# One layer of sparse attention and a state-space branch: Pool's front work on VectorE, and index scores in pieces of two PSUM banks and 2048 columns

## The chip, the cores and the metric

The kernel runs on one core of a Trainium2 chip, in one launch. The metric is the time of that launch on the device in microseconds. A core has five engines, each with its own queue of instructions worked off in order: TensorE (PE in the profile; PEld is its loading of weights), VectorE (DVE), ScalarE (ACT), Pool (POOL) and SyncE (SP), which only issues DMAs. They wait for one another by semaphores.

## What is computed

The layer takes x of 4096 positions by 1024 channels. Cut to what matters here, one projection gives the inputs of both branches, the attention branch selects 256 keys for each query, and both branches go through one output projection and a layer norm:

```python
proj = einsum('bsd,de->bse', x, w_in)
q, c_kv, q_idx, k_idx, w_idx, gate_a, u, gate_s = split(proj)
# index: 8 heads of 32 channels
idx_logits = einsum('bthd,bsd->bths', q_idx, k_idx)
index_score = einsum('bths,bth->bts', relu(idx_logits), w_idx)   # 4096 x 4096, causal
_, sel = top_k(index_score, 256)
# attention over the selected latents, 8 heads, keys and values absorbed
s = einsum('bthc,btkc->bthk', q_lat, c[sel]);  o_lat = softmax(s) @ c[sel]
# state-space branch: diagonal complex recurrence over positions, GELU, GLU
mixed = concat([att * silu(gate_a), ssm * silu(gate_s)])
out = layer_norm(2**0.25 * x + mixed @ w_out)
```

The kernel keeps float32 accuracy on TensorE by splitting an operand into a rounded high part and a remainder (hi and lo) and adding three products.

## The kernel before

The code is written as one stream, and a scheduler of the recording layer lays it out over the engines: for each engine it fixes an order in which instructions of later code stand between those of earlier code wherever it expects them to be ready. On the chip each queue then runs in that order.

**The first stage** holds two streams of work. The projections: `sweep(c, cols, following)` takes a chunk c of 512 positions through the 21 column blocks of COLS. Per block, 24 matmuls of 512 columns (`mm3`, L98 to L100) go to a PSUM tile ps_x (four of them), are evacuated through a staging tile `st` (four buffers) and stored to DRAM by SP. The first three blocks (index keys, index queries) run for all chunks at the start; the other 18 run later, chunk 7 first, which also rounds the weights into hi and lo (L498, L499) and stores them to w_d for the other chunks. Block ckv makes the normalised latent: it needs the squares (tile `sq`) and a diagonal matrix (L572, also `sq`). Block kv makes keys and values: 4 key pieces and 8 value pieces a chunk, each split into hi and lo by `split_pool`: ScalarE copies the PSUM tile twice, once rounded (L93) and once plain (L94), and Pool subtracts (L95). `prepare` transposes x for the next chunk and splits it with `split` (ScalarE rounds, L85, and VectorE subtracts straight out of PSUM, L87).

The selection: `select(group)` treats two to five tiles of 128 queries at once; tile i sees W = 128(i+1) keys. Tiles 0 and 1 need no selection. `score` (L233 to L258) computes the index scores: for each stretch of 1024 keys and each of 8 heads, two matmuls of 512 columns into PSUM tiles ps_i (four buffers of one bank), two relus on ScalarE (L248) into one tile `relu` of 1024 columns (four buffers), and one accumulation on VectorE (L257). Then eight rounds (L312 to L359) search each query's threshold: a count per tile, on VectorE (L321) or ScalarE (L317), and a dozen operations on a few columns. At the end of a group (L375 to L399), for each tile: ScalarE flips signs (L378), VectorE makes a mask of the entries above the threshold (L382), Pool adds it to the scores (L383), VectorE finds the eight largest of the rest and strikes them out (L385, L393), ScalarE turns the result into the mask (L397), and SP stores it. Score tiles of two groups fit, so a group's scoring lies beside the search of the one before it.

**The tail**: when the last group is selected, a check whether any row failed decides a branch; only then does the second stage begin.

**The second stage** is attention with the state-space branch between its instructions, then the output. Its code is not touched.

Pool's queue in the first stage also issues the loads of weights (L503) and of index queries (L238).

## Time and profile before

| | us |
|---|---|
| median of three runs | 4163.76 (4161.73 to 4170.51) |
| the profiled execution, whole | 4164.02 |
| its span, first to last instruction | 4162.0 |
| busy in the span: TensorE | 3715.5 |
| VectorE | 3445.4 |
| ScalarE | 2806.0 |
| Pool | 1907.0 |

Times in rows are counted from the start of the span. A row of lines names the source line, the engine, the operation, what it writes and reads, and the shape; then the count, the busy time in us and the mean of one instruction in ns; then the idle time of the engine just before these instructions, and what ended it. A line can be that of a helper: L87 is every subtraction of `split`. An instruction counts as busy from its start to its end, also while it stands still inside.

### The profile page before, as it was taken

The page shows a single profiled execution, that of the slowest core. Times are in us where ns is not written, and L with a number is a line of the kernel's source. Part 1 is how long each engine was busy: PE and PEld are TensorE (multiplying, and loading weights), DVE is VectorE, ACT ScalarE, POOL GpSimd, SP SyncE. Part 2 cuts the span into 40 slices and gives each one's busy share as a digit, 9 for nine tenths or more (in the row PEclk, how much of TensorE's full clock was granted, in tenths as well). Part 3 has the DMA queues.
Part 4 walks back from the last instruction along what each step waited for, and adds up shares of the span by engine and source line. Part 5 has one row for each costly group of instructions (what it writes and reads, how often), then busy time and mean ns, then how long its engine had stood idle before and what let it go on. Part 6 is the DMA issues. An engine that isn't in the chain of part 4 may idle for free.

```text
span 4162.0 us, 65556 instructions
## 1 busy us (share of the span) xinstructions
PE 3715.5 (89%) x20925; PEld 3123.2 (75%) x20925; DVE 3445.4 (83%) x7049; ACT 2806.0 (67%) x5100; POOL 1907.0 (46%) x3561
## 2 busy tenths in 40 slices
PE   6888988989889889319999999999999999899998
PEld 5666766766667667308988888889898989788887
DVE  4989999999998999859888888888888889665554
ACT  4677787766776767537777777777777778534342
POOL 1213443333332333336665757565657552344543
PEclk9898989989889999759999999999999999999999
DMA  8675867667676766434444544544545444544441
GB/s 230 156 203 165 269 187 222 188 190 210 169 213 180 210 198 188 123 100 125 130 134 130 147 134 140 134 132 127 138 119 153 114 137 134 164 141 139 136 128 71
DMA packets 521907, 656.26 MB, mean 158 GB/s; under 512 B 126800, under 2 KB 367952, under 8 KB 521552
## 3 DMA queue, kind: packets, MB, share of 16 engines
q1 hardware_dynamic: 438800, 448.54, 37.6%
q0 software_dynamic: 82752, 203.45, 18.2%
q8 instruction: 167, 2.74, 0.3%
q14 instruction: 188, 1.54, 0.1%
HBM read 480.61 MB, written 169.13 MB: 156 GB/s over the span
## 4 chain that ended last, share of the span: by engine, by line
PE 46%; ACT 3%; DMA 2%; DVE 1%; issue 1%; POOL 1%; SPq 0%; ACTq 0%; POOLq 0%; DVEq 0%
PE ps_t L1141 10%; PE ps_o L1153 6%; PE ps_o L1154 5%; PE ps_s L1108 5%; PE ps_s L1109 5%; PE ps_y L99 3%; PE ps_y L98 3%; PE ps_y L100 3%; ACT sc L1124 2%; PE ps L951 2%; PE ps_g L99 1%; PE ps_g L100 1%; PE ps_g L98 1%; DMA mb<-mask_d 1%; ACT ph L85 1%
## 5 line engine op out<-in xcount | busy, mean ns | idle before, releaser
L87 DVE TENSOR_TENSOR pl<-ps_t,ph 128x512 fp32r<-128x512 f32 x1088 | 748.2, 688 | 192.2 <-ACT ph L85 178.9
L85 ACT ACTIVATE ph<-ps_t 128x512 fp32r<-128x512 f32 x1088 | 643.6, 596 | 371.1 <-PE ps_t L1141 353.1
L1111 DVE CUSTOM_DVE_ANT_0 sc<-ps_s,mb 128x512 f32<-128x512 f32 (+3 forms) x1152 | 725.7, 638 | 38.4 <-PE ps_s L1109 19.4
L248 ACT ACTIVATE relu<-ps_i 128x512 f32<-128x512 f32 (+2 forms) x1136 | 586.2, 603 | 217.6 <-PE ps_i L247 146.8
L257 DVE SCALAR_TENSOR_TENSOR acc<-relu,wi,acc 128x1024 f32<-128x1024 f32 (+7 forms) x546 | 664.3, 1217 | 65.2 <-ACT relu L248 55.7
L1153 PE MATMUL ps_o<-ph,V 128*128 128x256 f32 x2176 | 658.7, 325 | 29.8 <-ACT ot L1157 26.8
L1141 PE MATMUL ps_t<-ident,sc 128*128 128x128 f32 x4352 | 654.5, 273 | 11.1 <-DVE pl L87 6.5
L1124 ACT ACTIVATE sc<-sc,mx 128x1024 f32<-128x1024 f32 (+7 forms) x640 | 636.9, 997 | 7.0 <-DVE mx L1111 6.3
L1141 PEld LDWEIGHTS ps_t<-ident,sc 128*128 128x128 f32 x4352 | 536.0, 141 | 123.2 <-DVE pl L87 7.3
L1154 PE MATMUL ps_o<-pl,V 128*128 128x256 f32 x2176 | 564.5, 281 | 2.6 <-DVE pl L87 2.6
L98 PE MATMUL ps_x<-xk,w 128*128 128x512 f32 x1280 | 524.2, 409 | 21.3 <-DMA w<-w_d 10.9
L247 PE MATMUL ps_i<-kst,qst 128*128 128x512 f32 (+1 forms) x1136 | 436.1, 456 | 101.9 <-ACT relu L248 97.5
L100 PE MATMUL ps_x<-xk,w 128*128 128x512 f32 x1280 | 511.4, 400 | 3.5 <-POOL w L499 3.3
L99 PE MATMUL ps_x<-xk,w 128*128 128x512 f32 x1280 | 511.0, 399 | 0.0
L503 POOL DMA_DIRECT2D w<-w_d x294 | 163.5, 556 | 680.6 <-PE ps_x L100 374.4
L1108 PE MATMUL ps_s<-KT,QH 128*128 128x512 f32 (+2 forms) x1152 | 438.2, 381 | 21.4 <-DMA QL<-qT_d 17.1
L1153 PEld LDWEIGHTS ps_o<-ph,V 128*128 128x128 f32 x2176 | 413.1, 190 | 47.1 <-ACT ot L1157 39.3
L1109 PE MATMUL ps_s<-KT,QL 128*128 128x512 f32 (+2 forms) x1152 | 436.2, 379 | 0.7 <-DVE QL L87 0.7
L1154 PEld LDWEIGHTS ps_o<-pl,V 128*128 128x128 f32 x2176 | 417.4, 192 | 7.3 <-DVE pl L87 3.3
L247 PEld LDWEIGHTS ps_i<-kst,qst 128*128 128x128 f32 x1136 | 232.7, 210 | 219.6 <-ACT relu L248 180.7
L317 ACT ACTIVATE junk_a<-acc,s_t 128x384 int8<-128x384 f32 (+13 forms) x128 | 273.3, 2135 | 92.3 <-DVE s_t L346 56.2
L98 PEld LDWEIGHTS ps_x<-xk,w 128*128 128x128 f32 x1280 | 248.7, 194 | 88.5 <-DMA w<-w_d 15.1
(410 smaller groups left out, 7916.7 us busy)
## 6 DMA issues: line engine op xcount, KB each, us to landing
w<-w_d POOLq DMA_DIRECT2D x294, 512.0 KB, 4.1
mb<-mask_d SPq DMA_DIRECT2D x416, 256.0 KB, 3.2
xs<-in_x_dram SPq DMA_DIRECT2D x120, 256.0 KB, 4.7
w_d<-w SPq DMA_DIRECT2D x42, 512.0 KB, 3.6
qs_d<-st SPq DMA_DIRECT2D x64, 256.0 KB, 3.4
k_d<-st SPq DMA_DIRECT2D x128, 128.0 KB, 3.0
v_d<-st SPq DMA_DIRECT2D x64, 256.0 KB, 3.6
KT<-k_d POOLq DMA_DIRECT2D x32, 512.0 KB, 4.5
```

The source lines that it names most:

```text
L85: ACT.activation(hi, src, AF.Copy, scale=scale)
L87: DVE.tensor_tensor(lo, src, ft(hi), op=OP.subtract)
L98: PE.matmul(ps, lh, rh, start=first, stop=False)
L99: PE.matmul(ps, lh, rl, start=False, stop=False)
L100: PE.matmul(ps, ll, rh, start=False, stop=last)
L247: PE.matmul(pi[:, :nn], qst[:, h, :], kst[:, s0 + q0:s0 + q0 + nn], start=True, stop=True)
L257: DVE.scalar_tensor_tensor(o, r, wi[:, i, h:h + 1], more, op0=OP.mult, op1=OP.add)
L1111: DVE.tensor_tensor_reduce(self.sc[a][-1][:, o], ps[:, :n], self.mb[a][:, o], 1.0, TOP, OP.add, OP.min, mx[:, k:k + 1])
L1124: ACT.activation(v, v, AF.Exp, scale=-1.0, bias=nm, accum_out=self.ds[:, a, r:r + 1])
L1141: PE.transpose(pt[:, e, a, :], self.sc[a][r][:, o:o + P], ident)
L1153: PE.matmul(self.po, v, ph_[:, e, :], start=(b + e == 0), stop=False)
L1154: PE.matmul(self.po, v, pl_[:, e, :], start=False, stop=(b + e == self.nb - 1))
```

## The change

Two things are changed together.

Pool's arithmetic of the first stage goes to VectorE. The masked add becomes a VectorE operation; key and value pieces use `split` in place of `split_pool`, which drops ScalarE's second copy, and VectorE subtracts out of PSUM; the weights' lo part and the diagonal are made by VectorE. Pool keeps its DMA issues and some small operations.

The index scores are cut differently. A PSUM tile ps_i has two banks (1024 columns) and there are two of them; two matmuls of 512 columns fill one, and one relu reads 1024 columns. A tile `relu` has 2048 columns, with three buffers, and one accumulation covers up to 2048 columns.

To make room, `st` gets three buffers and takes the place of `sq` as well; the outgoing mask `m` gets two buffers; the mask of the finish (`mk`) and the discarded output of VectorE's counts share one buffer.

```diff
-    WB = 3
+    WB, RW, RB = 3, 2048, 3
-    psi = idxs.enter_context(tc.tile_pool(name="i_ps", bufs=4, space=PSUM))
+    psi = idxs.enter_context(tc.tile_pool(name="i_ps", bufs=2, space=PSUM))
...
-        for s0 in range(0, W, 1024):
-            n = min(1024, W - s0)
+        for s0 in range(0, W, RW):
+            n = min(RW, W - s0)
             for h in range(HEADS):
-                r = wk.tile([P, 1024], FT, name="relu", bufs=4)
-                for q0 in range(0, n, C):
-                    m = min(C, n - q0)
-                    nn = (m + 255) // 256 * 256
-                    pi = psi.tile([P, C], FT, name="ps_i")
-                    PE.matmul(pi[:, :nn], qst[:, h, :], kst[:, s0 + q0:s0 + q0 + nn], start=True, stop=True)
+                r = wk.tile([P, RW], FT, name="relu", bufs=RB)
+                for q0 in range(0, n, 2 * C):
+                    m = min(2 * C, n - q0)
+                    pi = psi.tile([P, 2 * C], FT, name="ps_i")
+                    for b0 in range(0, m, C):
+                        nn = (min(C, m - b0) + 255) // 256 * 256
+                        PE.matmul(pi[:, b0:b0 + nn], qst[:, h, :], kst[:, s0 + q0 + b0:s0 + q0 + b0 + nn], start=True,
+                                  stop=True)
                     ACT.activation(r[:, q0:q0 + m], pi[:, :m], AF.Relu)
...
-                    junk = wk.tile([P, S], mybir.dt.uint8, name="junk_d", bufs=1)
+                    junk = wk.tile([P, PEN], BF, name="mk", bufs=1).bitcast(mybir.dt.uint8)
...
-                mk = wk.tile([P, PEN], BF, name="m", bufs=3)
+                mk = wk.tile([P, PEN], BF, name="mk", bufs=1)
                 DVE.tensor_scalar(mk[:, :c1 - c0], v[:, c0:c1], th[:, k:k + 1], -BIG, op0=OP.is_ge, op1=OP.mult)
-                POOL.tensor_tensor(v[:, c0:c1], v[:, c0:c1], mk[:, :c1 - c0], op=OP.add)
+                tt(v[:, c0:c1], v[:, c0:c1], mk[:, :c1 - c0], op=OP.add)
...
-                mk = wk.tile([P, PEN], BF, name="m", bufs=3)
+                mk = wk.tile([P, PEN], BF, name="m", bufs=2)
...
-                        (DVE if e < 3 else POOL).tensor_tensor(wk0[:, 1], wst, ft(wk0[:, 0]), op=OP.subtract)
+                        DVE.tensor_tensor(wk0[:, 1], wst, ft(wk0[:, 0]), op=OP.subtract)
...
-                    cf = sm.tile([P, C], FT, name="sq")
+                    cf = sm.tile([P, C], FT, name="st", bufs=3)
...
-                        kt = [sm.tile([P, C], FT, name="st", bufs=4).bitcast(FR) for _ in range(2)]
-                        split_pool(*kt, ps)
+                        kt = [sm.tile([P, C], FT, name="st", bufs=3).bitcast(FR) for _ in range(2)]
+                        split(*kt, ps)
...
-                            split_pool(st[:, :, 0:HD], st[:, :, HD:P], ps[:, hs])
+                            split(st[:, :, 0:HD], st[:, :, HD:P], ps[:, hs])
...
-                    sq = sm.tile([P, C], FT, name="sq")
+                    sq = sm.tile([P, C], FT, name="st", bufs=3)
...
-                    dg = sm.tile([P, 4, P], FT, name="sq")
+                    dg = sm.tile([P, 4, P], FT, name="st", bufs=3)
                     for a in range(4):
-                        POOL.tensor_scalar(dg[:, a, :], ident, rn[:, a:a + 1], None, op0=OP.mult)
+                        DVE.tensor_scalar(dg[:, a, :], ident, rn[:, a:a + 1], None, op0=OP.mult)
```

Lines of the changed kernel stand two further down from L248 on (L257 before is L259 after, L382 is L384).

How the queues change is seen at two places. The first is VectorE's queue at the end of a group, for tile 28 (3712 keys, so pieces of 2048 and 1664; m and mk are the masks, acc the scores, s_top the eight maxima). Before, VectorE's queue reads:

```order
L382 TENSOR_SCALAR m_6781<-acc_6094,s_t_6621 128x2048
L382 TENSOR_SCALAR m_6784<-acc_6094,s_t_6621 128x1664
L257 SCALAR_TENSOR_TENSOR acc_6823<-relu_7242,wi_103,acc_6823 128x1024
L257 SCALAR_TENSOR_TENSOR acc_6823<-relu_7250,wi_103,acc_6823 128x1024
L257 SCALAR_TENSOR_TENSOR acc_6823<-relu_7258,wi_103,tieb_104 128x512
L385 MAX s_top_6777<-acc_6094 128x8
L257 SCALAR_TENSOR_TENSOR acc_6823<-relu_7263,wi_103,acc_6823 128x512
L389 TENSOR_TENSOR eq0_113<-s_top_6777 128x7
L257 SCALAR_TENSOR_TENSOR acc_6823<-relu_7268,wi_103,acc_6823 128x512
L390 SCALAR_TENSOR_TENSOR s_eqj_6779,tf_161<-slot1_111,s_e_6625,eq0_113 128x8
```

Three accumulations of the next group's scores stand between the masks and the maxima, while Pool adds.

In the changed kernel VectorE's queue reads, at the end of the same group:

```order
L384 TENSOR_SCALAR mk_5885<-acc_5390,s_t_5725 128x2048
L385 TENSOR_TENSOR acc_5390<-acc_5390,mk_5885 128x2048
L384 TENSOR_SCALAR mk_5888<-acc_5390,s_t_5725 128x1664
L385 TENSOR_TENSOR acc_5390<-acc_5390,mk_5888 128x1664
L259 SCALAR_TENSOR_TENSOR acc_5927<-relu_6188,wi_103,acc_5927 128x1536
L387 MAX s_top_5881<-acc_5390 128x8
L384 TENSOR_SCALAR mk_5908<-acc_5389,s_t_5725 128x2048
L259 SCALAR_TENSOR_TENSOR acc_5927<-relu_6197,wi_103,acc_5927 128x1536
L391 TENSOR_TENSOR eq0_113<-s_top_5881 128x7
L385 TENSOR_TENSOR acc_5389<-acc_5389,mk_5908 128x2048
```

Each mask is now followed by its add (L385 of the changed kernel), and of the three accumulations one is left ahead of the maxima.

The second place is ScalarE's and VectorE's queue where a chunk's key pieces are split, beside the scoring of tile 30. ScalarE before, with two copies for each key piece:

```order
L93 ACTIVATE st<-ps_x 128x512
L94 ACTIVATE st<-ps_x 128x512
L248 ACTIVATE relu<-ps_i 128x512
L248 ACTIVATE relu<-ps_i 128x384
L93 ACTIVATE st<-ps_x 128x512
L94 ACTIVATE st<-ps_x 128x512
L248 ACTIVATE relu<-ps_i 128x512
L248 ACTIVATE relu<-ps_i 128x384
L248 ACTIVATE relu<-ps_i 128x512
L248 ACTIVATE relu<-ps_i 128x384
```

Between the copies stand the relus, one for each PSUM bank.

ScalarE in the changed kernel, beside the same scores:

```order
L250 ACTIVATE relu<-ps_i 128x1024
L250 ACTIVATE relu<-ps_i 128x896
L250 ACTIVATE relu<-ps_i 128x1024
L250 ACTIVATE relu<-ps_i 128x896
L85 ACTIVATE st<-ps_x 128x512
L250 ACTIVATE relu<-ps_i 128x1024
L250 ACTIVATE relu<-ps_i 128x896
L85 ACTIVATE st<-ps_x 128x4x64
L250 ACTIVATE relu<-ps_i 128x1024
```

Two copies of a key piece (L93, L94) have become one (L85), and pairs of relus of 512 and 384 columns have become one of 896, beside one of 1024.

VectorE before, at the accumulations that belong to these relus:

```order
L257 SCALAR_TENSOR_TENSOR acc<-relu,wi,tieb 128x896
L87 TENSOR_TENSOR xk<-ps_x,xk 128x512
L359 TENSOR_TENSOR s_t<-s_t,s_n 128x4
L257 SCALAR_TENSOR_TENSOR acc<-relu,wi,acc 128x896
L321 TENSOR_SCALAR junk_d,s_t<-acc,s_t 128x1664
L257 SCALAR_TENSOR_TENSOR acc<-relu,wi,acc 128x896
L321 TENSOR_SCALAR junk_d,s_t<-acc,s_t 128x2560
L257 SCALAR_TENSOR_TENSOR acc<-relu,wi,acc 128x896
L323 TENSOR_TENSOR s_t<-s_t,cm 128x4
L257 SCALAR_TENSOR_TENSOR acc<-relu,wi,acc 128x896
```

The accumulations alternate with the search of the group before; the subtractions of the key pieces are in Pool's queue.

VectorE in the changed kernel, at the same tile's last stretch:

```order
L259 SCALAR_TENSOR_TENSOR acc<-relu,wi,tieb 128x1920
L87 TENSOR_TENSOR st<-ps_x,st 128x512
L298 BN_STATS s_st<-acc 128x6
L343 TENSOR_TENSOR s_d<-s_ab 128x8
L259 SCALAR_TENSOR_TENSOR acc<-relu,wi,acc 128x1920
L87 TENSOR_TENSOR st<-ps_x,st 128x512
L299 BN_AGGR s_mv<-s_st 128x2
L344 RECIPROCAL s_e<-s_d 128x4
L259 SCALAR_TENSOR_TENSOR acc<-relu,wi,acc 128x1920
L87 TENSOR_TENSOR st<-ps_x,st 128x512
L345 TENSOR_TENSOR s_e<-s_e,s_ab 128x4
L259 SCALAR_TENSOR_TENSOR acc<-relu,wi,acc 128x1920
```

One subtraction of a key piece (L87 on st) now stands ahead of each accumulation of 1920 columns.

## Rows read from the trace of the kernel before

**Rows 1.** Busy us by stretch: PE, PEld, DVE, ACT, POOL, then TensorE's clock

```profile
60.00:1707.00 1647.00, 1444.82 (x5762) 1093.68 (x5761) 1507.16 (x2513) 1185.37 (x2058) 543.77 (x566) 0.91 0.71 198
1600.00:1700.00 100.00, 98.39 (x427) 79.26 (x425) 86.04 (x110) 69.94 (x112) 33.47 (x36) 1.00 0.72 211
1707.00:1846.00 139.00, 0.40 (x4) 0.12 (x2) 104.62 (x237) 53.43 (x62) 48.23 (x52) 0.51 0.14 44
1846.00:4162.00 2316.00, 2236.57 (x15008) 2003.92 (x15008) 1807.80 (x4184) 1544.55 (x2943) 1305.87 (x2862) 0.99 0.48 134
```

**Rows 2.** Waits, 60 to 1700 us: total us, times, longest us

```profile
DVE acc L257 <- ACT relu L248: 60.0, 52, 4.0
DVE xk L87 <- ACT xk L85: 14.0, 6, 4.5
PE ps_i L247 <- ACT relu L248: 97.1, 73, 6.2
```

**Rows 3.** Lines of POOL, 0 to 1860 us: count | busy us, mean ns | idle before

```profile
L383 POOL TENSOR_TENSOR acc<-acc,m 128x2048 f32<-128x2048 f32 (+15 forms) x46 | 153.3, 3335 | 74.2 <-DVE m L382 59.6 <-DVE s_e L342 4.0 <-DVE s_n L334 2.6
L95 POOL TENSOR_TENSOR st<-st 128x256 fp32r<-128x256 f32 (+1 forms) x96 | 119.0, 1252 | 127.7 <-ACT st L94 87.4 <-DMA xs<-in_x_dram 18.2 <-issue 15.7
L499 POOL TENSOR_TENSOR w<-xs,w 128x512 fp32r<-128x512 f32 x36 | 51.1, 1423 | 66.9 <-ACT w L498 54.1 <-DMA xs<-in_w_uv_dram 6.6 <-DMA w_d<-w 3.2
L572 POOL TENSOR_SCALAR sq<-ident,rn 128x128 f32<-128x128 f32 x32 | 33.4, 1054 | 52.7 <-DVE rn L569 36.6 <-PE ps_i L247 16.0
```

**Rows 4.** Timeline around 1166 us, VectorE and Pool: start us, us

```profile
1168.28 8.14 DVE L257 SCALAR_TENSOR_TENSOR acc<-relu,wi,acc 128x1024 f32<-128x1024 f32 x2 [2.57 <-ACT relu L248]
1166.51 7.43 POOL L383 TENSOR_TENSOR acc<-acc,m 128x2048 f32<-128x2048 f32 x2
```

**Rows 5.** One line's instructions: duration ns min/median/max, first and last start us

```profile
L257 DVE SCALAR_TENSOR_TENSOR acc<-relu,wi,acc x546: 301/1276/6755, 70.0 to 1713.1; 128x1024 f32<-128x1024 f32 x122, 128x384 f32<-128x384 f32 x10, 128x640 f32<-128x640 f32 x10, 128x768 f32<-128x768 f32 x9
L499 DVE TENSOR_TENSOR w<-xs,w x6: 680/691/692, 26.0 to 38.2; 128x512 fp32r<-128x512 f32 x6
L258 DVE TENSOR_TENSOR acc<-acc,capm x30: 251/291/3591, 79.8 to 1714.4; 128x128 f32<-128x128 f32 x30
L325 DVE TENSOR_SCALAR s_b<-s_t x80: 138/164/10729, 181.2 to 1783.1; 128x2 int32<-128x2 f32 x40, 128x4 int32<-128x4 f32 x24, 128x5 int32<-128x5 f32 x8, 128x3 int32<-128x3 f32 x8
L95 POOL TENSOR_TENSOR st<-st x12: 722/1454/2260, 536.1 to 563.1; 128x256 fp32r<-128x256 f32 x8, 128x512 fp32r<-128x512 f32 x4
```

**Rows 6.** Lines of VectorE, 0 to 1860 us

```profile
L257 DVE SCALAR_TENSOR_TENSOR acc<-relu,wi,acc 128x1024 f32<-128x1024 f32 (+7 forms) x546 | 664.3, 1217 | 65.2 <-ACT relu L248 55.7 <-DVE s_t L324 0.4
L257 DVE SCALAR_TENSOR_TENSOR acc<-relu,wi,tieb 128x1024 f32<-128x1024 f32 (+4 forms) x78 | 103.7, 1329 | 5.0 <-ACT relu L248 4.3 <-ACT m L397 0.2
L325 DVE TENSOR_SCALAR s_b<-s_t 128x2 int32<-128x2 f32 (+3 forms) x80 | 32.4, 405 | 1.0
L326 DVE TENSOR_SCALAR s_b<-s_t 128x2 int32<-128x2 f32 (+3 forms) x80 | 13.4, 168 | 0.0
L343 DVE TENSOR_TENSOR s_e<-s_e,s_ab 128x2 f32<-128x2 f32 (+3 forms) x70 | 23.6, 337 | 1.5
L345 DVE TENSOR_TENSOR s_e<-s_e,s_d 128x2 f32<-128x2 f32 (+3 forms) x70 | 14.6, 208 | 1.5
L258 DVE TENSOR_TENSOR acc<-acc,capm 128x128 f32<-128x128 f32 x30 | 14.4, 479 | 0.2
L385 DVE MAX8 s_top<-acc 128x8 f32<-128x384 f32 (+29 forms) x30 | 74.6, 2486 | 13.2 <-POOL acc L383 13.2
```

**Rows 7.** DMA issues: KB each, median us to landing

```profile
v_d<-st SPq DMA_DIRECT2D x64, 256.0 KB, 3.6
```

**Rows 8.** Lines of ScalarE, 0 to 1860 us, L248 by shape

```profile
L93 ACT ACTIVATE st<-ps_x 128x256 fp32r<-128x256 f32 (+1 forms) x96 | 49.4, 515 | 18.2 <-DMA v_d<-st 10.4 <-DMA k_d<-st 3.9 <-PE ps_i L247 1.6
L248 ACT ACTIVATE relu<-ps_i 128x512 f32<-128x512 f32 x960 | 535.9, 635 | 182.8 <-PE ps_i L247 119.7 <-DVE acc L257 28.2 <-DVE eq L389 16.2
L248 ACT ACTIVATE relu<-ps_i 128x256 f32<-128x256 f32 x56 | 22.1, 414 | 13.7 <-PE ps_i L247 8.7 <-DVE acc L257 5.0
```

More of the change, by code (lines that the diff above doesn't have):

```diff
@@ L264, in causal_only @@
         W = P * (i + 1)
-        m = wk.tile([P, PEN], BF, name="m", bufs=3)
+        m = wk.tile([P, PEN], BF, name="m", bufs=2)
         if W > P:
@@ L410, in count @@
                 W = P * (i + 1)
-                junk = wk.tile([P, S], mybir.dt.uint8, name="junk_d", bufs=1)
+                junk = wk.tile([P, PEN], BF, name="mk", bufs=1).bitcast(mybir.dt.uint8)
                 t = thr if isinstance(thr, float) else thr[:, k:k + 1]
@@ L434, in select_any @@
             v = xs[k][:, :W]
-            eq = wk.tile([P, S], mybir.dt.uint8, name="junk_d", bufs=1)[:, :W]
+            eq = wk.tile([P, PEN], BF, name="mk", bufs=1).bitcast(mybir.dt.uint8)[:, :W]
             m = wk.tile([P, ROOM], FT, name="acc", bufs=4)
@@ L524, in sweep @@
                             hs = slice(4 * r, 4 * r + 4)
-                            st = sm.tile([P, 4, P], FT, name="st", bufs=4).bitcast(FR)
-                            split_pool(st[:, :, 0:HD], st[:, :, HD:P], ps[:, hs])
+                            st = sm.tile([P, 4, P], FT, name="st", bufs=3).bitcast(FR)
+                            split(st[:, :, 0:HD], st[:, :, HD:P], ps[:, hs])
                             SP.dma_start(v_d[hs, :, 4 * c + a, :].rearrange("h p v -> p h v"), ft(st))
@@ L539, in sweep @@
                         PE.matmul(p2, sell[:, h, :], ql, start=False, stop=True)
-                        st = sm.tile([P, C], FT, name="st", bufs=4)
+                        st = sm.tile([P, C], FT, name="st", bufs=3)
                         ACT.activation(st, p2, AF.Copy)
@@ L544, in sweep @@
                 elif n == "kw":
-                    kwf = sm.tile([P, C], FT, name="st", bufs=4)
+                    kwf = sm.tile([P, C], FT, name="st", bufs=3)
                     DVE.tensor_copy(kwf, ps)
@@ L559, in sweep @@
                 elif n == "ckv":
-                    craw = sm.tile([P, C], FT, name="st", bufs=4)
+                    craw = sm.tile([P, C], FT, name="st", bufs=3)
                     ACT.activation(craw, ps, AF.Copy)
-                    sq = sm.tile([P, C], FT, name="sq")
+                    sq = sm.tile([P, C], FT, name="st", bufs=3)
                     ACT.activation(sq, ps, AF.Square)
@@ L577, in sweep @@
                 else:
-                    st = sm.tile([P, C], FT, name="st", bufs=4)
+                    st = sm.tile([P, C], FT, name="st", bufs=3)
                     rows = slice(j * P, (j + 1) * P)
@@ L1017, in tile_hymba @@
     DVE.tensor_reduce(lo1[:, NG:], lo1[:, :NG], axis=AX.X, op=OP.add)
-    pl = psi.tile([P, C], FT, name="ps_i")
+    pl = psi.tile([P, 2 * C], FT, name="ps_i")
     PE.matmul(pl[:1, :NG + 1], ones[:, 0:1], lo1, start=True, stop=True)
```

## The prediction

> **What bounds the kernel now.** I read the busy time by stretch first. The program has two stages with a short tail between them [rows 1]. From 60 to 1707 us the projections and the index selection run together; from 1707 to 1846 us only the last group's selection is left and TensorE does nothing; from 1846 us on comes attention, where TensorE is busy 2236.6 of 2316 us and which the change does not touch. In the first stage VectorE is busy 1507.2 of 1647 us, TensorE 1444.8, ScalarE 1185.4. TensorE's figure is stretched: its granted clock there is 0.91 in the mean, and where it is 1.00, from 1600 to 1700 us, 427 matmuls take 98.4 us. 5762 matmuls at that pace are 5762 x 98.4/427 = 1328 us. So VectorE is the bound of the first stage, and alone in the tail. The waits agree [rows 2]: VectorE's longest is 60.0 us for the relus, small against 1507.
>
> Next I asked what VectorE's time is made of. Pool's four kinds of work that the change moves take 153.3 + 119.0 + 51.1 + 33.4 = 357 us of Pool [rows 3], and they lie beside VectorE's work, so at first sight they are free. They are not. From 1166.51 us Pool runs two masked adds in 7.43 us; VectorE starts two accumulations at 1168.28 us and needs 8.14 us for them, where the median of this instruction is 1.276 us [rows 4, 5]. VectorE stands still inside its instruction until Pool is through, and the longest accumulation took 6.755 us. The busy time of VectorE therefore holds stalls.
>
> **What the stalls are worth.** A clean price first. Two-input operations out of SBUF: medians of 0.691 us for 512 columns and 0.291 us for 128 [rows 5], so 1.04 ns a column and 0.16 us fixed. The accumulation at 1024 columns, 1.276 us, is then 1.065 us of columns and 0.21 us fixed. Tiles 2 to 31 have 128 x (3 + ... + 32) = 67,200 columns, 8 heads make 537,600. Clean, the 546 + 78 = 624 accumulations would take 559 + 624 x 0.21 = 690 us; they took 664.3 + 103.7 = 768 [rows 6]. Stalls: 78 us. The small operations of the search show the same thing: L325 and L326 do the same operation on the same shape 80 times each, 32.4 against 13.4 us, L326 starting when the stall of L325 is over. Of these 19 us one stall of 10.7 us (L325's maximum) lies in the tail beside Pool's preparation of the state-space batches, which stays, so 8 go. Seven more groups of small operations, from L343 (mean 337 ns) down to L345 (208 ns), stand above L326's 168 ns and hold 45 us between them. L258 has 0.479 in the mean against 0.291: 30 x 0.19 = 6 us. Sum 137 us; with a tenth for the groups too small to list I take **150 us** (137 at the least; 165 would be every such stall).
>
> **The change part by part**, as time of VectorE.
> Removed: the stalls, -150. Longer accumulations: pieces of 2048 make 14 x 8 + 16 x 2 x 8 = 368 instructions of 624, so 256 x 0.21 = -54.
> Added: the masked adds, 46 of them over 67,200 columns: 46 x 0.16 + 70 = +77 (80 if they cost what an accumulation costs). The weights' low parts, 36 x 0.69 = +25. The key halves 32 x 0.69 = +22. The value halves, 64 of 256 columns at 0.16 + 0.27 = 0.43: +27. The diagonal, 32 x 128 columns, between 0.16 (L326) and 0.29 (L258): +6. Together +157.
> So VectorE's own work changes by -150 - 54 + 157 = **-47 us**: the moved work costs nearly what the stalls cost, and the gain is about the fixed cost of the shorter pieces.
>
> Waits. VectorE waited 13.2 us for Pool's masked add before it could look for the maxima [rows 6]; the add now stands in its own queue: -13. New are the waits of 96 + 36 splits for ScalarE's high half, which Pool bore until now. The 120 splits of x cost 14.0 us of such waits [rows 2], 0.117 each: +15. Behind a split that waits, the accumulations of the next group are queued, as the order shows.
> The staging tile has three buffers for four, and now also serves the squares and the diagonal. One chunk's key and value splits ran from 536.1 to 563.1 us, 27 us for 16 staging tiles [rows 5], and a store of one lands after 3.6 us [rows 7]. If the landings set that pace, three buffers need 4/3 of it: 9 us, 72 in eight chunks. But where ScalarE writes their first halves it waited only 10.4 + 3.9 us in all for these landings [rows 8], so they set it seldom. Bounds 0 and 72; I take +10, nearer to the row of waits.
> ScalarE loses the second of two equal passes of each key and value split, -49 [rows 8], and 1136 - 624 = 512 relus. By 635 ns at 512 and 414 at 256 columns [rows 8] a relu has 193 ns fixed, so -99. VectorE's 60 us of waiting for relus should shrink with a ScalarE that has 148 of 1185 us less to do; against that the first accumulation of a row now needs two relus of 1024. Bounds -40 and +30; I take -15.
> The two-bank PSUM tiles change no matmul count; junk and mask buffers that become one are written and read by VectorE in order and cost nothing.
>
> Sum: -47 - 13 + 15 + 10 - 15 = **-50 us**, all of it in the 1785 us before attention. The profiled execution took 4164.0 us (span 4162.0), the median is 4163.8, so nothing has to be corrected: **4114 us**.
>
> **The rivals.**
> *VectorE gains and TensorE or ScalarE takes it back.* TensorE waited 97.1 us for relus at the score matmuls [rows 2]. With two PSUM tiles of two banks, two matmuls wait for one relu of 1024 columns, and the sweep's matmuls stand behind them in order. If that adds 40 us of idle time to VectorE, 4154 us. For it: the coarser grain. Against it: TensorE needs 1328 of 1647 us, and PSUM holds as many columns as before. The Trainium skill ("Perfetto Trace Analysis", Optimizing Scalar/DVE Operations) advises breaking instructions up where an engine that isn't saturated causes bubbles on another, which ScalarE does here; by it the larger relus lose.
> *VectorE's idle time shrinks too.* In the first stage it idles 140 us, mostly for ScalarE and matmuls that were themselves late because VectorE stalled for 3 to 7 us at a time. If a third of that goes and all 165 us of stalls do: -50 - 15 - 40, about 4060 us.
> *The staging buffers decide (slower).* All three are held when the squares and the diagonal of a chunk are made, and keys need two at a time. If VectorE's splits stand for each landing: 72 us, and one landing more for each latent chunk, 8 x 3.6 = 29. Then -60 + 72 + 29 = +41: 4205 us. It turns slower once these waits pass 60 us.
> *The stalls stay.* If the long accumulations had another cause than Pool, VectorE gets 157 - 54 - 13 = 90 us more: 4254 us. The Trainium skill (same page and section) says that for a saturated VectorE moving work off it, even to GpSimd, may make sense; this change does the opposite, and by that rule alone it loses these 90 us. The same section adds that the two share a read port, so that it might not help; the row of 6.755 us shows which holds here. That the moves aren't made can be excluded: the order has 46 masked adds and 96 more splits on VectorE.
>
> **How the numbers follow.** Chances: forecast (4085 to 4145) 0.50; TensorE or ScalarE takes it back (4145 to 4172) 0.16; idle time shrinks too (4040 to 4085) 0.16; staging buffers 0.16; stalls stay 0.02. A measurement of this kernel can tell 0.2%, 8 us, from no change. Faster by more than that: the forecast, the shrinking, and half of the second case, 0.74. Within it: the other half and the mildest tenth or so of the buffer case, 0.10. Slower: 0.16. The range takes in both sides of the forecast and the milder half of the buffer case: 4050 to 4180 us.
>
> **What would show it right or wrong.** Right: accumulations of 2048 columns near 0.21 + 2.13 = 2.34 us with hardly one above 2.5; L326's twin at 0.17 us; VectorE's work between 60 us and attention near 1565 us, where the two rows of before add up to 1612; attention as long as before. Wrong: VectorE waiting more than 60 us at the key and value splits or for relus; accumulations still at 3 us and more; or a first stage in which TensorE is the one that never waits.

## The result

The changed kernel took 4134.95 us (median of 4 runs, 4132.23 to 4140.52), the kernel before, run beside it, 4167.14. The ratio is 0.9925 with a 95% interval of 0.9907 to 0.9944: 32 us faster, where 50 were forecast. The profiled execution took 4132.33 us, with a span of 4130.5.

Its busy time by stretch, with the columns of [rows 1]: the first stage until the last score matmul, the tail until the check for failed rows, and attention with all behind it. The last line is the kernel before, its tail until the check.

```profile
60.00:1690.70 1630.70, 1415.14 (x5758) 1075.39 (x5756) 1447.82 (x2452) 1118.58 (x1452) 208.26 (x374) 0.91 0.72 200
1690.70:1807.00 116.30, 3.17 (x6) 1.66 (x6) 108.02 (x252) 56.27 (x59) 19.13 (x29) 0.51 0.19 57
1821.50:4130.00 2308.50, 2238.44 (x15008) 2005.04 (x15008) 1806.23 (x4184) 1543.05 (x2942) 1302.35 (x2857) 0.99 0.47 134
1707.00:1838.00 131.00, 0.40 (x4) 0.12 (x2) 104.62 (x237) 53.43 (x62) 45.72 (x46) 0.51 0.14 45
```

From the check to the end both kernels take some 2324 us (4130.5 − 1807 and 4162.0 − 1838), so all of the gain lies ahead of it. From 60 us to the check VectorE's work adds up to 1447.82 + 108.02 = 1556 us and the stretch to 1747, which leaves 191 us idle. Before, the check began at 1838 us: a stretch of 1778, 1612 of work, 166 idle. **Work fell by 56 us, idle time rose by 25.** The forecast had 47 and a fall of 3.

The lines of VectorE that answer to [rows 6] (numbers two further down; the adds, splits and weights are new on this engine):

```profile
L259 DVE SCALAR_TENSOR_TENSOR acc<-relu,wi,acc 128x2048 f32<-128x2048 f32 (+15 forms) x322 | 558.6, 1735 | 50.9 <-ACT relu L250 47.3 <-DVE s_t L326 0.4
L259 DVE SCALAR_TENSOR_TENSOR acc<-relu,wi,tieb 128x2048 f32<-128x2048 f32 (+15 forms) x46 | 79.8, 1736 | 14.9 <-ACT relu L250 13.0 <-ACT m L399 1.4
L385 DVE TENSOR_TENSOR acc<-acc,mk 128x2048 f32<-128x2048 f32 (+15 forms) x46 | 77.1, 1676 | 0.4
L87 DVE TENSOR_TENSOR st<-ps_x,st 128x256 fp32r<-128x256 f32 (+1 forms) x96 | 47.2, 506 | 13.2 <-DMA k_d<-st 6.7 <-ACT st L85 6.5
L384 DVE TENSOR_SCALAR mk<-acc,s_t 128x2048 bf16<-128x2048 f32 (+15 forms) x46 | 45.1, 980 | 23.0 <-ACT acc L380 22.9
L501 DVE TENSOR_TENSOR w<-xs,w 128x512 fp32r<-128x512 f32 x42 | 28.7, 686 | 11.4 <-ACT w L500 11.1
L327 DVE TENSOR_SCALAR s_b<-s_t 128x2 int32<-128x2 f32 (+3 forms) x80 | 13.9, 173 | 1.7
L328 DVE TENSOR_SCALAR s_b<-s_t 128x2 int32<-128x2 f32 (+3 forms) x80 | 13.4, 168 | 0.0
L260 DVE TENSOR_TENSOR acc<-acc,capm 128x128 f32<-128x128 f32 x30 | 8.6, 287 | 0.1
L574 DVE TENSOR_SCALAR st<-ident,rn 128x128 f32<-128x128 f32 x32 | 7.1, 280 | 0.0
```

And the accumulation's durations, as in [rows 5] (min/median/max in ns):

```profile
L259 DVE SCALAR_TENSOR_TENSOR acc<-relu,wi,acc x322: 339/1946/2354, 70.7 to 1696.0; 128x2048 f32<-128x2048 f32 x70, 128x384 f32<-128x384 f32 x7, 128x640 f32<-128x640 f32 x7, 128x896 f32<-128x896 f32 x7
```

The stalls are gone: no accumulation took over 2.354 us, where 6.755 was the longest before at half the width, and L327, the twin of L328, costs 13.9 us and not 32.4. The waits that answer to [rows 2]:

```profile
DVE acc L259 <- ACT relu L250: 60.3, 52, 5.6
DVE mk L384 <- ACT acc L380: 22.5, 8, 4.1
PE ps_i L248 <- ACT relu L250: 116.1, 132, 4.5
DVE s_t L325 <- ACT junk_a L319: 15.9, 14, 2.5
```

and the wait for the sign flip in the kernel before:

```profile
DVE m L382 <- ACT acc L378: 7.6, 5, 2.0
```

VectorE waits as long for relus as before, although ScalarE has less to do; a wait for ScalarE's sign flip (L380) has grown from 7.6 to 22.5 us; and TensorE waits 116.1 us for relus, before 97.1. The question for the experiments is where this idle time comes from, and which half of the change earns the 32 us.

### The profile page after: what moved, and what is told of

The parts are those of the page before. It is cut to its first block, busy times and chain, and to the rows that moved or that the text cites. A ratio compares the mean times of both kernels' runs of the same rounds, so it can differ in the third digit from the quotient of the medians.

```text
span 4130.5 us, 64310 instructions
## 1 busy us (share of the span) xinstructions
PE 3692.4 (89%) x20925; PEld 3108.8 (75%) x20925; DVE 3387.9 (82%) x7003; ACT 2741.9 (66%) x4492; POOL 1542.2 (37%) x3351
## 4 chain that ended last, share of the span: by engine, by line
PE 45%; ACT 3%; DMA 2%; issue 2%; DVE 2%; POOL 2%; SPq 0%; ACTq 0%; POOLq 0%; DVEq 0%
PE ps_t L1143 10%; PE ps_o L1155 6%; PE ps_o L1156 5%; PE ps_s L1110 5%; PE ps_s L1111 5%; PE ps_y L99 2%; PE ps_y L98 2%; PE ps_y L100 2%; ACT sc L1126 2%; PE ps L953 2%; PE ps_g L99 1%; PE ps_g L100 1%; PE ps_g L98 1%; ACT ph L85 1%; DMA mb<-mask_d 1%
## 5 line engine op out<-in xcount | busy, mean ns | idle before, releaser
L87 DVE TENSOR_TENSOR pl<-ps_t,ph 128x512 fp32r<-128x512 f32 x1088 | 748.9, 689 | 191.3 <-ACT ph L85 177.3
L85 ACT ACTIVATE ph<-ps_t 128x512 fp32r<-128x512 f32 x1088 | 643.6, 596 | 370.9 <-PE ps_t L1143 349.0
L250 ACT ACTIVATE relu<-ps_i 128x1024 f32<-128x1024 f32 (+5 forms) x624 | 533.9, 895 | 211.4 <-PE ps_i L248 175.2
L259 DVE SCALAR_TENSOR_TENSOR acc<-relu,wi,acc 128x2048 f32<-128x2048 f32 (+15 forms) x322 | 558.6, 1735 | 50.9 <-ACT relu L250 47.3
L98 PE MATMUL ps_x<-xk,w 128*128 128x512 f32 x1280 | 517.8, 405 | 8.0 <-ACT w L500 2.4
L248 PE MATMUL ps_i<-kst,qst 128*128 128x512 f32 (+1 forms) x1136 | 398.7, 449 | 124.7 <-ACT relu L250 116.1
L99 PE MATMUL ps_x<-xk,w 128*128 128x512 f32 x1280 | 505.8, 395 | 0.0
L100 PE MATMUL ps_x<-xk,w 128*128 128x512 f32 x1280 | 504.8, 395 | 0.0
L248 PEld LDWEIGHTS ps_i<-kst,qst 128*128 128x128 f32 x1136 | 221.8, 213 | 241.4 <-ACT relu L250 202.9
```

What stands on the lines that cost most here:

```text
L85: ACT.activation(hi, src, AF.Copy, scale=scale)
L87: DVE.tensor_tensor(lo, src, ft(hi), op=OP.subtract)
L98: PE.matmul(ps, lh, rh, start=first, stop=False)
L99: PE.matmul(ps, lh, rl, start=False, stop=False)
L100: PE.matmul(ps, ll, rh, start=False, stop=last)
```

## The experiments

The table collects what is shown below: medians, the ratio to the kernel before beside each, and VectorE's work and idle time from 60 us to the check, worked out from rows by stretch as above. Work and idle time are those of one profiled execution, which lies up to 10 us from the median (e2 4201, e3 4154, e10 4187; the others within 4).

| kernel | us | ratio, 95% interval | work | idle |
|---|---|---|---|---|
| before | 4166 to 4168 | 1 | 1612 | 166 |
| the change | 4135 | 0.9925 (0.9907, 0.9944) | 1556 | 191 |
| e1: moves | 4143 | 0.9946 (0.9933, 0.9958) | 1584 | 171 |
| e2: pieces and buffers | 4210 | 1.0106 (1.0091, 1.0122) | 1573 | 244 |
| e3: masked add alone | 4162 | 0.9987 (0.9977, 0.9996) | 1589 | 178 |
| e4: the other moves alone | 4179 | 1.0032 (1.0019, 1.0044) | 1596 | 196 |
| e9: moves, 3 staging buffers | 4123 | 0.9900 (0.9886, 0.9915) | 1584 | 153 |
| e7: the change, one-bank relus | 4129 | 0.9910 (0.9897, 0.9923) | 1560 | 181 |
| e8: the change, accumulations of 1024 | 4146 | 0.9952 (0.9935, 0.9968) | 1590 | 172 |
| e10: before, 3 staging buffers | 4177 | 1.0026 (1.0017, 1.0036) | 1610 | 182 |
| new layout of before | 4179 | 1.0027 (1.0017, 1.0038) | 1607 | 185 |
| new layout of the change | 4140 | 0.9936 (0.9922, 0.9950) | 1558 | 193 |
| new layout of e9 | 4124 | 0.9898 (0.9884, 0.9912) | 1581 | 155 |
| new layout of e1 | 4150 | 0.9963 (0.9950, 0.9977) | 1581 | 178 |

### Moves and pieces apart

e1 is the kernel before with Pool's work on VectorE and nothing else:

```diff
-                POOL.tensor_tensor(v[:, c0:c1], v[:, c0:c1], mk[:, :c1 - c0], op=OP.add)
+                tt(v[:, c0:c1], v[:, c0:c1], mk[:, :c1 - c0], op=OP.add)
-                        (DVE if e < 3 else POOL).tensor_tensor(wk0[:, 1], wst, ft(wk0[:, 0]), op=OP.subtract)
+                        DVE.tensor_tensor(wk0[:, 1], wst, ft(wk0[:, 0]), op=OP.subtract)
-                        split_pool(*kt, ps)
+                        split(*kt, ps)
-                            split_pool(st[:, :, 0:HD], st[:, :, HD:P], ps[:, hs])
+                            split(st[:, :, 0:HD], st[:, :, HD:P], ps[:, hs])
-                        POOL.tensor_scalar(dg[:, a, :], ident, rn[:, a:a + 1], None, op0=OP.mult)
+                        DVE.tensor_scalar(dg[:, a, :], ident, rn[:, a:a + 1], None, op0=OP.mult)
```

> The kernel before with Pool's four kinds of work on VectorE and nothing else changed (pieces, PSUM tiles and buffers as before). Theory 1, the forecast's sum: the stalls that go (-150) and the work that comes (+157) cancel, -13 for the tail's wait and +15 for the splits' waits cancel too, so 4155 to 4170 us against 4167; the gain of the changed kernel comes from its longer pieces. Theory 2: the moves bring the whole gain, because a stall costs more than its own length, and the longer pieces bring only idle time: 4125 to 4140 us.

e2 is the rest of the change (all its lines but those five): pieces of 2048, relus over two banks, the smaller buffers, and Pool's work left on Pool. The masks that Pool adds share the two buffers of `m` with the outgoing ones.

> The changed kernel with the moves undone: longer accumulations, two-bank relus, three staging buffers, two mask buffers, and Pool works as before. Theory 1: 256 fixed costs of 0.21 us less, -54, less some waits: 4115 to 4135 us. Theory 2: the longer pieces save VectorE time that it then idles away waiting for relus and matmuls: 4160 to 4180 us.

Measured: 4143 and 4210 us. Both lie outside the ranges of both theories. The moves bring 22 us; the pieces, with the smaller buffers, cost 44 when they come alone. In e2 the accumulations wait far longer, and so does TensorE (from 60 us to the check at 1877):

```profile
DVE acc L259 <- ACT relu L250: 119.5, 65, 6.1
PE ps_i L248 <- ACT relu L250: 148.7, 131, 7.4
DVE s_top L387 <- POOL acc L385: 26.4, 9, 5.5
DVE m L384 <- DMA mask_d<-m: 13.1, 6, 5.0
```

VectorE's work in e2 is 39 us less than before and its idle time 78 us more. The accumulations' wait for relus is 60 us longer, the wait for Pool's add 13; another 13 are a wait for a mask to be stored, which before was 0.2 us (two mask buffers instead of three). The sign of the second term of the forecast, longer accumulations as a plain gain, is already in doubt.

e3 and e4 split the five lines of e1: e3 has the masked add (the first) alone, e4 the other four.

> The kernel before with the masked add alone on VectorE. By rows of before: the stalls beside the masked add (some 90 us) and the wait of 13 us go, 77 us of adds come: about -25, 4142 us. If what VectorE loses to Pool's add was free time anyway, +50 or more: 4215 us and above.

> The kernel before with the splits of keys, values and weights and the diagonal on VectorE, the masked add left on Pool. Stalls beside these (some 60 to 70 us) go, 80 us of work and 17 us of waits come: about +25, 4192 us. Rival: ScalarE's second pass of 49 us that goes with it counts in full, and it comes out below 4155 us.

Measured: 4162 and 4179 us, −3 and +14, together −22. Neither time is in a range that was expected. Each half takes away some 20 us of VectorE's work (1612 to 1589 and 1596) and has 12 and 30 us more idle time. The work shows what each does to the stalls. The moved instructions, by their durations in the changed kernel less an overlap that is worked out further down, should add an estimated 73 us in e3 and 66 in e4. So some 1612 + 73 − 1589 = 96 us of stalls are gone in e3 and 1612 + 66 − 1596 = 82 in e4. Together that is no less than the 167 that go with both (estimated in the same way, below): each half takes its own stalls away. That the time doesn't follow is due to the idle time. Why it rises is open; a new layout alone moved it by 19 us (below).

### Staging, relus, accumulations

e9 is e1 with the staging of the change, three buffers that also serve the squares and the diagonal; e10 is the kernel before with that staging.

```diff
-                    cf = sm.tile([P, C], FT, name="sq")
+                    cf = sm.tile([P, C], FT, name="st", bufs=3)
...
-                        st = sm.tile([P, C], FT, name="st", bufs=4)
+                        st = sm.tile([P, C], FT, name="st", bufs=3)
```

> The moves of Pool's work alone (old pieces of 1024 columns, one-bank relus), but with three staging buffers that also serve the squares and the diagonal, as in the change. It is compared with the moves alone with four buffers and squares apart, 4143 us. Theory: staging costs little, and the idle time that the whole change gained over the moves (156 to 183 us in the first stage) comes from the longer pieces: 4138 to 4150 us. Rival: the three staging buffers make that idle time, as VectorE's splits of keys and values stand for the landings: 4155 to 4175 us, with waits of VectorE and ScalarE at the staging tile 12 to 30 us longer.

> The kernel before, with only the staging tiles cut from four to three buffers that also serve the squares and the diagonal; pieces, relus and Pool's work as before. The new pieces without the moves took 44 us more than before; this tells whether the staging did. Theory 1: the longer pieces did, since a stalled accumulation now holds twice the columns and the relus come late: here 4160 to 4175 us. Theory 2: the staging did, because Pool's splits hold a staging tile longer than VectorE's: 4190 to 4215 us.

e7 is the change with relus of one bank:

```diff
-    psi = idxs.enter_context(tc.tile_pool(name="i_ps", bufs=2, space=PSUM))
+    psi = idxs.enter_context(tc.tile_pool(name="i_ps", bufs=4, space=PSUM))
-                for q0 in range(0, n, 2 * C):
-                    m = min(2 * C, n - q0)
-                    pi = psi.tile([P, 2 * C], FT, name="ps_i")
+                for q0 in range(0, n, C):
+                    m = min(C, n - q0)
+                    pi = psi.tile([P, C], FT, name="ps_i")
...
```

> The whole change, but with relus of 512 columns over one PSUM bank (four tiles of one bank, as before) and accumulations of 2048 columns kept. It is compared with the whole change, 4135 us. Theory 1: the accumulations of 2048 columns make VectorE wait (it must have four relus before it can begin), two banks don't matter for that, and ScalarE's 512 relus more, about 99 us of its time, are mostly hidden: 4130 to 4145 us. Theory 2: the two-bank tiles are at fault, since two matmuls wait for one relu of 1024 columns: 4105 to 4125 us, TensorE's wait for relus back from 116 to 97 us. Theory 3: ScalarE's time counts nearly in full once Pool's stalls are gone: 4150 to 4190 us.

e8 is the change with accumulations of 1024:

```diff
-    WB, RW, RB = 3, 2048, 3
+    WB, RW, RB = 3, 1024, 6
```

> The whole change, but with accumulations of 1024 columns and six relu buffers of 1024, the relus of 1024 over two banks kept. It is compared with the whole change, 4135 us. Theory 1: the longer accumulations bring 256 x 0.133 = 34 us of VectorE's time and lose most of it to idle time (27 us more than with the moves alone): here 4130 to 4145 us, VectorE's first-stage busy time about 30 us higher and its idle time about 25 us lower, near 157. Theory 2: the relus over two banks make the idle time and the longer accumulations are a clean gain: 4155 to 4175 us, idle time stays near 183.

Measured: **e9 takes 4123 us, less than the whole change**; nothing expected that. e10 takes 4177, 9 more than the kernel before beside it: the staging isn't what made e2 slow. e7 and e8 take 4129 and 4146, each within 2 us of the range of its first theory, that the long accumulations make VectorE wait. On top of e9, accumulations of 2048 (e7) cost 6 us, relus over two banks (e8) 23, both (the change) 12. All three also have the change's mask buffers (two for `m`, one shared by `mk` and the discarded counts) where e9 has those of before; their traces show no wait for a mask to be stored longer than 0.7 us, but no run separates these buffers from the cutting. e9's rows by stretch and lines:

```profile
60.00:1674.90 1614.90, 1440.23 (x5765) 1096.86 (x5765) 1471.17 (x2713) 1161.35 (x1970) 211.07 (x375) 0.90 0.73 202
1674.90:1797.00 122.10, 0.05 (x2) 0.08 (x2) 113.04 (x246) 50.79 (x53) 18.93 (x28) 0.50 0.14 46
```

```profile
L257 DVE SCALAR_TENSOR_TENSOR acc<-relu,wi,acc 128x1024 f32<-128x1024 f32 (+7 forms) x546 | 605.0, 1111 | 45.3 <-ACT relu L248 39.5
L257 DVE SCALAR_TENSOR_TENSOR acc<-relu,wi,tieb 128x1024 f32<-128x1024 f32 (+4 forms) x78 | 86.9, 1114 | 14.0 <-ACT relu L248 9.7 <-ACT m L397 4.0
```

```profile
DVE m L382 <- ACT acc L378: 7.7, 5, 2.9
PE ps_i L247 <- ACT relu L248: 76.6, 78, 6.4
DVE acc L257 <- ACT relu L248: 49.1, 65, 3.3
DVE s_t L323 <- ACT junk_a L317: 10.1, 8, 3.7
```

The waits sort the four kernels that have the moves and three staging buffers. TensorE's wait for relus was 76.6 us in e9 and 81.2 in e7 (one bank), 102.4 in e8 and 116.1 in the change (two banks). VectorE's wait for the sign flip was 7.7 us in e9 and 13.6 in e8 (accumulations of 1024), 20.6 in e7 and 22.5 in the change (2048). But e1, with relus of one bank, accumulations of 1024 and four staging buffers, has

```profile
PE ps_i L247 <- ACT relu L248: 98.7, 80, 5.2
DVE m L382 <- ACT acc L378: 6.3, 6, 2.5
```

So with the moves the flip's wait goes with the long accumulations, but two banks aren't needed for a long wait of TensorE, and that they cause it in e8 and the change isn't shown.

The waits of VectorE account for most of the 38 us of idle time that the change has more than e9: 15 for the flip, 11 at the accumulations for relus (49.1 to 60.3), 6 for the counts of ScalarE (10.1 to 15.9).

How the wait for the flip arises is seen where the group with tiles 30 and 31 ends. First the change, ScalarE and then VectorE:

```profile
979.96 1.03 ACT L250 ACTIVATE relu<-ps_i 128x1024 f32<-128x1024 f32 x1 [1.93 <-PE ps_i L248]
980.88 7.21 ACT L380 ACTIVATE acc<-acc,s_sg 128x3968 f32<-128x3968 f32 x2
987.99 0.80 ACT L250 ACTIVATE relu<-ps_i 128x768 f32<-128x768 f32 x1
```

```profile
984.52 1.28 DVE L384 TENSOR_SCALAR mk<-acc,s_t 128x2048 bf16<-128x2048 f32 x1 [4.11 <-ACT acc L380]
985.84 2.29 DVE L385 TENSOR_TENSOR acc<-acc,mk 128x2048 f32<-128x2048 f32 x1
988.17 1.22 DVE L384 TENSOR_SCALAR mk<-acc,s_t 128x1920 bf16<-128x1920 f32 x1
989.30 2.08 DVE L259 SCALAR_TENSOR_TENSOR acc<-relu,wi,acc 128x1792 f32<-128x1792 f32 x1
```

The relu of 1024 columns is done at 980.99 us, but it is half of a piece: the accumulation of 1792 columns needs the relu of 768 as well, which stands behind two sign flips. VectorE sits 4.11 us with finished work before it that it can't take up. The same place in e9, VectorE:

```profile
963.97 1.28 DVE L257 SCALAR_TENSOR_TENSOR acc<-relu,wi,acc 128x1024 f32<-128x1024 f32 x1
967.47 2.42 DVE L382 TENSOR_SCALAR m<-acc,s_t 128x2048 bf16<-128x2048 f32 x2 [2.21 <-ACT acc L378]
```

Here an accumulation of 1024 fills the first 1.3 us of the flip, and 2.21 are left.

### The same work in another order

All these kernels differ in their layout too: the scheduler orders every queue anew after each edit, and e9's TensorE queue differs from e1's in thousands of lines, though only buffers differ. So four kernels were run with two tiny operations of the group's end, neither of which reads the other, written in reverse. The work is the same, the layout isn't.

```diff
-        ts(sg, low, 2.0, -1.0, op0=OP.mult, op1=OP.add)
         ts(sc, low, 1.5, -1.0, op0=OP.mult, op1=OP.add)
+        ts(sg, low, 2.0, -1.0, op0=OP.mult, op1=OP.add)
```

> The kernel before, with two tiny operations at the end of a group (sg and sc, a few columns each, neither reads the other) written in the other order. The work is the same to the last instruction, but the scheduler lays the queues out anew: TensorE's differs in some 5100 rows of 16275. It measures what a new layout alone is worth. Theory: layout alone moves the time by 8 to 25 us either way, so that the single parts of the change (moves alone, three staging buffers, two-bank relus) can't each be read as the price of their mechanism: 4140 to 4158 or 4174 to 4190 us. Rival: layout alone is worth under 6 us, and the parts' prices are real: 4160 to 4172 us.

> The changed kernel with the same two tiny operations in the other order; the same work, TensorE's queue differs in some 5500 rows of 16192. Theory of the layout: 8 to 25 us away from the changed kernel's 4135, so 4110 to 4127 or 4143 to 4160 us. Rival: within 6 us, 4129 to 4141 us.

> The moves with three staging buffers and the old pieces (4123 us), with the same two tiny operations in the other order; the same work, TensorE's queue differs in some 7400 rows of 16279. Theory of the layout: the 4123 us was a lucky layout, as the moves with four buffers (4143 us) did the same work in another; here 4131 to 4148 us. Rival: three buffers are really better with the moves, and the new pieces really cost 12 us: 4117 to 4129 us.

> The moves alone with four staging buffers and squares apart (4143 us), with the same two tiny operations in the other order: the same work, TensorE's queue differs in some 4500 rows of 16286. The two layouts of the moves with three buffers took 4123 and 4124 us. Theory: the 20 us between four and three buffers were the layout, so staging has no price and the moves alone are worth some 40 us: here 4115 to 4135 us. Rival: with the moves, four buffers really are slower than three, and the moves alone are worth some 22 us: 4138 to 4150 us.

Measured: +11 us for the kernel before, +5 for the change, 0 for e9, +7 for e1. The kernel before moved as far as the theory said, the other three stayed within the ranges of the rivals. A layout was worth up to 11 us in these four pairs, so single steps of that size in the table (e3, e7 against e9, e10) prove nothing, and e4's +14 little. What repeats in both layouts weighs more: e9 at 4123 and 4124 is ahead of the change at 4135 and 4140, and of e1 at 4143 and 4150. The split of VectorE's time repeats too: idle time 153 and 155 in e9, 191 and 193 in the change, at 28 and 23 us more work in e9. What doesn't repeat is the rise of idle time from before to the change: 25 us in the first layouts, 8 in the second (185 to 193). The change's second layout shows the same waits:

```profile
DVE mk L384 <- ACT acc L380: 22.8, 8, 6.3
PE ps_i L248 <- ACT relu L250: 105.4, 140, 4.3
```

e9's second layout has 6.4 and 76.8 us for these two, e1's 4.7 and 110.4. At the accumulations VectorE waits 67.5 us for relus in the change's second layout and 49.7 in e9's.

Left open: why three staging buffers are some 20 us better than four with the moves, in two layouts each, and not better without them (4177 against 4168 and 4179). VectorE's work is the same, its idle time is 18 and 23 us less, spread over many lines; no single wait of VectorE carries it. What does change in both layouts is TensorE's wait for relus, 98.7 to 76.6 us and 110.4 to 76.8; whether that is cause or effect no run tells. Only one layout of e7 and of e8 was run, so the split of the 12 us between the two halves of the cutting is open as well.

## Why the prediction was right, and where it wasn't

The forecast was 4114 us, faster, with 4085 to 4145 as its own range, and 4135 came. Its sum was nearer than its parts, and that was luck. It gave the pieces −54 and most of −15 for the relus, and the moves with their waits and the staging +19 (−150 + 157 − 13 + 15 + 10). The runs give **the moves with the staging −44** (e9, 4123 against 4168 beside it) and **the pieces on top of them +12**, +16 in the other layout. Two errors of some 60 and 80 us cancelled in part.

- **What bounds the kernel, right in the main.** VectorE's work fell by 56 us and the time by 32; attention didn't change. ScalarE doesn't bound it: from e9 to the change its work fell by 37 us and the time rose by 12. But TensorE stands close behind. The forecast counted 1328 us for it, at the pace of a stretch with a granted clock of 1.00; in e9's first stage the clock is 0.90 in the mean and TensorE is busy 1440 of 1615 us, VectorE 1471.
- **Stalls −150, right, a little small.** VectorE's work fell from 1612 us before to 1584 in e9, while some 156 us of moved work came in, less 17 for an overlap (both below). So the stalls that went are an estimated 1612 + 156 − 17 − 1584 = 167 us. The clean price of all accumulations was put at 690 us; in e9 they took 605.0 + 86.9 = 691.9, where 768 stood before. L260, L258 before, has a mean of 0.287 us, before 0.479. The step "which stays" failed: the stall of 10.7 us in the tail beside Pool's preparation is gone, since L327's 80 instructions took 13.9 us in all; why, no run shows. Pool still prepares these batches in the tail, from 1701 us on; the worst stalls of VectorE beside them are 1.79 and 2.27 us.
- **Added work +157, right by duration**: 77.1 us for the adds (77 forecast), 47.2 for the key and value halves (49), 24.7 for 36 of the 42 weight pieces (25), 7.1 for the diagonal (6).
- **Fixed costs −54, mis-sized: the step 256 x 0.21.** By duration it is right to the us: 691.9 − 638.4 = 53.5. But VectorE's work fell by only 28 us (23 in the other layout). Instructions of this engine overlap, so that the durations of a row count more than the time they occupy. Two back-to-back accumulations of 1024 before, and one of 2048 with its successor in the change:

```profile
876.17 2.47 DVE L257 SCALAR_TENSOR_TENSOR acc<-relu,wi,acc 128x1024 f32<-128x1024 f32 x2
878.56 0.15 DVE L341 TENSOR_TENSOR s_d<-s_ab 128x4 f32<-128x4 f32 x1
```

```profile
714.51 2.35 DVE L259 SCALAR_TENSOR_TENSOR acc<-relu,wi,tieb 128x2048 f32<-128x2048 f32 x1
716.77 2.21 DVE L259 SCALAR_TENSOR_TENSOR acc<-relu,wi,acc 128x1920 f32<-128x1920 f32 x1
```

  From start to start two of 1024 take 878.56 − 876.17 = 2.39 us and one of 2048 takes 2.26: a merge saves 0.13 us, 256 of them 33. The Trainium skill says as much ("Perfetto Trace Analysis", Optimizing Scalar/DVE Operations): its overheads are times for which the engine is busy, and the latency in a profile is about twice that, since half overlaps with the next instruction. The trace agrees on the overlap, but its 0.13 is about double the page's 60 ns for VectorE on SBUF; the measurement decides. The same overlap of some 0.08 us makes the 210 added instructions an estimated 17 us cheaper than their durations. That is half of the 35 us by which VectorE's work with the moves alone came out below the forecast (+7 forecast, −28 in e9); the other half is the stalls.
- **ScalarE's relus −99, mis-sized in the same way**: the step 512 x 0.193. The relus' total fell only from 586.2 us before (L248) to 533.9 (L250), and by the distance from start to start the merges save still less. Four relus of 512 with their successor in e9 and one of 1024 with its successor in the change, ScalarE:

```profile
970.91 2.07 ACT L248 ACTIVATE relu<-ps_i 128x512 f32<-128x512 f32 x4
972.82 0.65 ACT L589 ACTIVATE st<-ps_x 128x512 f32<-128x512 f32 x1
```

```profile
989.15 1.04 ACT L250 ACTIVATE relu<-ps_i 128x1024 f32<-128x1024 f32 x1
990.06 0.61 ACT L591 ACTIVATE st<-ps_x 128x512 f32<-128x512 f32 x1
```

  From start to start four of 512 take 972.82 − 970.91 = 1.91 us, so two take 0.955, against 990.06 − 989.15 = 0.91 for one of 1024: some 0.045 us saved, 512 of them 23. ScalarE's busy time from 60 us to the check fell by 37 us from e9 to the change (1161.35 + 50.79 against 1118.58 + 56.27).
- **Waits: −13 right but replaced, +15 about right, +10 wrong, −15 wrong.** The wait for Pool's add (13.2 us) is gone, but the sign flip's wait stands there now, 22.5 us. The key and value splits wait 6.5 us for ScalarE and 6.7 for landings, the weights' splits 3.7 for ScalarE from 60 us on. Staging costs nothing that the runs with the moves show: there three buffers are some 20 us faster than four, for a reason that stays open. The wait for relus is 60.3 where it should have shrunk.
- **The first rival came half true.** VectorE's idle time rises by 38 us from e9 to the change in both layouts, where the rival said 40. Its path is shown only in part: 15 us of the 38 are the wait for the flip, which the rival didn't have, and TensorE's wait for relus is long in e1 too, without two banks. Against it the forecast set that "PSUM holds as many columns as before"; that was true and didn't prevent the idle time. The sentence of the Trainium skill weighed there advises breaking instructions up where an engine that isn't saturated causes bubbles on another. The trace agrees in that the smaller pieces (e9) are ahead by 12 and 16 us and VectorE idles less. The second rival, idle time that shrinks with the stalls, isn't seen: e1, without the stalls, idles 171 and 178 us in its two layouts, the kernel before 166 and 185. e9's 153 and 155 came with the staging.
- **The signs named for "right"** came (2.35 us for 2048, 1556 us of work for 1565, L327 at 0.173); of those for "wrong", VectorE's wait for relus, 60.3 us and 67.5 in the other layout, is past its bound of 60.

## What to carry to other kernels

Price a merge of instructions by the distance from start to start of two that stand back to back, not by their durations, and set against it what the larger piece makes wait: here the new cutting saved some 28 us of VectorE's work and cost 38 of idle time. Work that stalls the engine which bounds the kernel isn't free because it lies on another engine: 357 us of Pool's work cost VectorE an estimated 167 us of stalls, and doing it itself some 139 (156 − 17). A sum that comes out right isn't a proof of its terms: run the halves of a change apart. Where a scheduler lays every queue out anew after an edit, run a harmless reordering of the same work first, and believe no step smaller than what that moves.

## What was unexpected of the hardware

- Both halves of Pool's large operations stall VectorE, and moving either leaves the stalls of the other: with the masked add moved alone the accumulations L257 on acc took 635.5 us, with the other moves alone 658.2, with both 605.0, before 664.3 [rows 6].
- A masked add of 2048 columns takes 2.29 us on VectorE, whereas Pool needed 7.43 us for one of 2048 and one of 1664 [rows 4]; 46 of them took 77.1 against 153.3 us [rows 3].
- Overlap of neighbours: about 0.08 us on VectorE (1.28 to 1.20 for 1024 columns) and about 0.12 us on ScalarE (0.60 to 0.48 for a relu of 512).
